# Seven block products for the down projections of two feed-forwards

## The chip, the cores and the metric

The kernel runs on one core of a Trainium2 chip. The metric is device time in microseconds (us), the median of several executions. TensorE (PE) does the matmuls, VectorE (DVE) and ScalarE (ACT) the elementwise work, GpSimd (POOL) little here, and SyncE's queue (SP) starts most of the transfers.

## The reference

One decoder layer on 512 tokens of width 1024, all in float32. The parts that matter here are the two feed-forwards, each with inner width 2816:

```
def swiglu(x, w_gate, w_up, w_down):
    return (jax.nn.silu(x @ w_gate) * (x @ w_up)) @ w_down

h = h + 0.5 * swiglu(rmsnorm(h, ffn1_norm), ffn1_w_gate, ffn1_w_up, ffn1_w_down)
... # mixer: sliding-window attention and gated linear attention, then h = h + concat(...) @ w_out
h = h + 0.5 * swiglu(rmsnorm(h, ffn2_norm), ffn2_w_gate, ffn2_w_up, ffn2_w_down)
h = h + sigmoid(rmsnorm(h, ple_gate_norm) @ ple_w_gate) * rmsnorm(p @ ple_w_proj, ple_norm)
```

## The kernel before

Every float32 factor of a large matmul is held as two float32r parts, high and low, whose sum is the value. A product is three matmuls (`mm3`): high x high, high x low, low x high. One matmul is 128 rows of contraction by 128 stationary columns by 512 moving columns, and accumulates in a PSUM bank of 512 float32 columns. There are eight banks, in three sets: `psA` (2), `psT` (4), `psG` (2).

Weights come through the class `Weights`. A list of units, in the order of use, is loaded by SP into raw tiles (two buffers of 128 x 2048), and each raw tile is split into ring tiles of 128 x 1024: ACT casts the high part (L87, `whi`), DVE subtracts it to get the low part (L88, `wlo`). The ring holds five high and five low tiles. A cast into a ring tile waits until PE has finished with the tile that had the slot. `get` asks for splits up to four units ahead of the one it returns.

`ffn` goes through the 22 blocks of 128 inner columns in three groups of 8, 8 and 6 (`GROUPS`). For each pair of blocks it computes gate and up for all 512 tokens, 24 matmuls for each of the four (8 contraction blocks x 3), into the four `psT` banks. The output has the inner columns on the partitions. Then `silu` on ACT (L267), the product with up on DVE (L269, `af`), the cast of the high part on ACT (L272, `ahi`), and the low part on DVE (L273, `alo`). At the end of a group comes the down projection: for each half of 512 output columns and each of the four token tiles, all blocks of the group accumulate in one `psA` bank, and one DVE instruction (L286) adds half of it to `h`. In the last group, `done(t)` follows a token tile's second half: it normalises the tile for the next stage, and the norm's transposes on PE come one tile later.

The program is written in order of use; a builder then fixes each engine's order of instructions by that order and by the times at which it reckons their inputs to be there. On the chip every engine takes its queue in that order.

Of the kernel before, what the change touches and what calls it, by code (L numbers as in the profile page):

```python
# [8 lines left out]
F32 = mybir.dt.float32  # L9
# [6 lines left out]
P = 128  # L16
# [9 lines left out]
GROUPS = ((0, 8), (8, 16), (16, 22))  # L26


class Weights:
    """Streams weight units from DRAM and splits each into two float32r parts whose sum is the float32 weight."""  # L30

    def __init__(self, nc, rawp, ringp, ahead):
        self.nc, self.rawp, self.ringp, self.ahead = nc, rawp, ringp, ahead
        self.units, self.where, self.tiles = [], {}, {}
        self.done = self.loaded = 0
        self.raws = []

# [5 lines left out]
    def add_cols(self, name, w, c0, nf):  # L43
        """[1024, nf*128] columns: one ring tile [P, 8, 128] per 128 columns."""
        keys = [(name, c0 // P + i) for i in range(nf)]
        src = w[:, c0:c0 + nf * P].rearrange("(k p) c -> p k c", p=P)
        self.add(keys, [P, KC, nf * P], [(slice(0, P), src)], [
            (lambda r, i=i: r[:, :, i * P:(i + 1) * P]) for i in range(nf)])

    def add_rows(self, name, w, k0, nk, c0, n, tag=None):  # L50
        """nk row blocks of 128 by n columns: one ring tile [P, 2, n] per two row blocks."""
        src = w[k0 * P:(k0 + nk) * P, c0:c0 + n].rearrange("(k p) c -> p k c", p=P)
        keys = [(name, c0 if tag is None else tag, k0 + i) for i in range(0, nk, 2)]
        self.add(keys, [P, nk, n], [(slice(0, P), src)], [
            (lambda r, i=i: r[:, i:i + 2, :]) for i in range(0, nk, 2)])

    def load(self):
        nc = self.nc
        keys, shape, loads, views = self.units[self.loaded]
        n = shape[1] * shape[2]  # L60
        u = self.loaded
        self.loaded += 1
        raw_t = self.rawp.tile([P, 2048], F32, name=f"wraw{u}", tag="wraw")
        raw = raw_t[:, :n].rearrange("p (k c) -> p k c", k=shape[1])
        for sl, src in loads:
            d = raw
            if isinstance(sl, tuple):
                d, sl = raw[:, :, sl[1]], sl[0]
            self.last_dma = nc.sync.dma_start(out=d[sl], in_=src).ins
        self.raws.append(raw)  # L70

    def split(self):
        nc = self.nc
        u = self.done
        while self.loaded <= u:
            self.load()
        keys, shape, loads, views = self.units[u]
        raw = self.raws[u]
        self.done += 1
        for i, (k, view) in enumerate(zip(keys, views)):  # L80
            v = view(raw)
            a, b = v.shape[1], v.shape[2]
            hi_t = self.ringp.tile([P, 1024], F32R, name=f"whi{u}_{i}", tag="whi")
            lo_t = self.ringp.tile([P, 1024], F32R, name=f"wlo{u}_{i}", tag="wlo")
            hi = hi_t[:, :a * b].rearrange("p (a b) -> p a b", a=a)
            lo = lo_t[:, :a * b].rearrange("p (a b) -> p a b", a=a)
            nc.scalar.copy(hi, v)  # L87
            (nc.gpsimd if u in (2, 3) else nc.vector).tensor_tensor(lo, v, hi.bitcast(F32), op=ALU.subtract)  # L88
            self.tiles[k] = (hi, lo)
# [8 lines left out]
def hymba_kernel(tc, A, out):  # L98
# [30 lines left out]
    def mm3(o, l, r, start, stop_):  # L129
        """o += l.T @ r where l and r are (hi, lo) pairs."""  # L130
        mm(o, l[0], r[0], start, False)
        mm(o, l[0], r[1], False, False)
        mm(o, l[1], r[0], False, stop_)

# [1 line left out]
    idn = cst.tile([P, P], F32, name="idn")  # L136
    make_identity(nc, idn)
    nhalf = cst.tile([P, 16], F32, name="nhalf")
# [13 lines left out]
    def add_ffn(i):  # L152
        g, u, d = A[f"ffn{i}_w_gate"], A[f"ffn{i}_w_up"], A[f"ffn{i}_w_down"]
        for f0, f1 in GROUPS:
            for f in range(f0, f1, 2):
                W.add_cols(f"g{i}", g, f * P, 2)
                W.add_cols(f"u{i}", u, f * P, 2)
            for c0 in (0, 512):
                for f in range(f0, f1, 4):
                    W.add_rows(f"d{i}", d, f, min(4, f1 - f), c0, 512)  # L160
# [84 lines left out]
    def ffn(i, nT, p, done, rest=None):  # L245
        first = True
        for f0, f1 in GROUPS:
            acts = {}
            for fa in range(f0, f1, 2):
# [4 lines left out]
                for a, b in halves:  # L254
                    if first and a and rest:
                        rest()
                    for j in range(2):
                        for m in range(2):
                            wh, wl = wts[j][m]
                            for k in range(KC):  # L260
                                mm3(pss[j][m][:, a:b], (wh[:, k, :], wl[:, k, :]),
                                    (nT[0][:, k, a:b], nT[1][:, k, a:b]), k == 0, k == KC - 1)
                first = False
                for j, f in enumerate(fs):
                    pg, pu = pss[j]
                    sg = p.tile([P, S], F32, name=f"sg{i}_{f}", tag="sg", bufs=2)
                    nc.scalar.activation(sg, pg, AF.Silu)  # L267
                    af = p.tile([P, S], F32, name=f"af{i}_{f}", tag="af", bufs=2)
                    nc.vector.tensor_mul(af, pu, sg)  # L269
                    ahi = p.tile([P, S], F32R, name=f"ahi{i}_{f}", tag="ahi", bufs=8)  # L270
                    alo = p.tile([P, S], F32R, name=f"alo{i}_{f}", tag="alo", bufs=8)
                    nc.scalar.copy(ahi, af)  # L272
                    nc.vector.tensor_sub(alo, af, ahi.bitcast(F32))  # L273
                    acts[f] = (ahi, alo)
            for c0 in (0, 512):
                tiles = [W.get((f"d{i}", c0, f)) for f in range(f0, f1, 2)]
                for t in range(NT):
                    ps = psA(f"pd{i}_{f0}_{c0}_{t}")
                    for j, (wh, wl) in enumerate(tiles):
                        for q in range(2):  # L280
                            f = f0 + 2 * j + q
                            ah, al = acts[f]
                            mm3(ps, (ah[:, tokens(t)], al[:, tokens(t)]), (wh[:, q, :], wl[:, q, :]),
                                f == f0, f == f1 - 1)
                    hs = h[t][:, c0:c0 + 512]
                    nc.vector.scalar_tensor_tensor(hs, ps, 0.5, hs, ALU.mult, ALU.add)  # L286
                    if c0 and f1 == NF:
                        done(t)

# [86 lines left out]
    with tc.tile_pool(name="ffn1p", bufs=1, reuse_waits="tile") as fp:  # L376
# [12 lines left out]
        ffn(1, nT1, fp, after1)  # L389

# [14 lines left out]
    def head_scale(src, name):  # L405
        """Per row and head of 64: (sum of squares + 64 eps) ** -0.5"""
# [7 lines left out]
    def rotate(x, tab, wide, name):  # L414
        """Rotary embedding of x (views by wide) with the gains folded into the tables."""
# [9 lines left out]
    # keys, values and gate ranks of all tokens  # L425
# [21 lines left out]
    # log decays of the recurrence and their running sums within chunks of 128 tokens  # L447
# [27 lines left out]
    # sliding-window attention; query heads are kept as pairs (h, h + 4), one per key head  # L475
# [73 lines left out]
    # gated linear attention  # L549
# [32 lines left out]
    # decayed scores of each chunk, transposed, by halving: pairs split at the middle of blocks of 2s tokens  # L582
# [51 lines left out]
    # decayed queries, keys and the state after each chunk  # L634
# [135 lines left out]
    hp = hpool.enter_context(tc.tile_pool(name="hp2", bufs=1, reuse_waits="tile"))  # L770
    h = [hp.tile([P, D], F32, name=f"h2_{t}") for t in range(NT)]
    for t in range(NT):
        nc.gpsimd.dma_start(out=h[t], in_=h_d[t])
    with tc.tile_pool(name="ffn2p", bufs=1, reuse_waits="tile") as fp:
        g2 = gain_tile("ffn2_norm")
        nT2 = norm_pair(fp, "f2")
# [13 lines left out]
        nT3 = norm_pair(xp, "pg")  # L790
# [7 lines left out]
        ffn(2, nT2, fp, after2, lambda: norm_transpose(*pend2[NT - 1]))  # L798

# [32 lines left out]
def _constants():  # L832
    """Tables that depend on the shapes alone: rotary angles and masks."""
# [46 lines left out]
```

## Time and profile before

| | before |
|---|---|
| median of 3 runs | 1035.73 us (1035.29 to 1036.16) |
| profiled execution, first to last instruction (its span) | 1034.1 us |
| PE busy | 1020.0 us |
| DVE busy | 457.8 us |
| ACT busy | 352.9 us |

The profile records one execution, and gives its time as the span alone; the difference of 1.6 us to the median is what lies around the span. Matmuls are pipelined: the profile's duration of one (some 390 ns) is longer than the step from one to the next, so that the step is read from a run of many.

### The profile page before, as it was taken

The numbers are of one execution on the slowest core, as the hardware profiler recorded it, in microseconds if no ns is written. First come the engines' busy times: TensorE is split into PE (matmuls) and PEld (weight loads), VectorE is DVE, ScalarE is ACT, GpSimd is POOL, SyncE is SP. The second block draws the span as 40 slices with busy tenths as digits, with TensorE's granted clock in tenths as the row PEclk, the third lists the DMA queues.
The fourth block names the chain that finished last, engine by engine and source line by source line (L and its number), as shares of the span: only waits on it lengthen the run. The fifth ranks groups of instructions, "written<-read, shape, count | busy, mean of one in ns | idle before, by whom it ended". The sixth has DMA issues, their size and how long they took to land.

```text
span 1034.1 us, 12380 instructions
## 1 busy us (share of the span) xinstructions
PE 1020.0 (99%) x5210; PEld 840.9 (81%) x5210; DVE 457.8 (44%) x610; ACT 352.9 (34%) x559; POOL 45.9 (4%) x58
## 2 busy tenths in 40 slices
PE   7999999999999999999999999999999999999998
PEld 5988888888888889887667779888888888888887
DVE  5533224333343346577876464332343323432553
ACT  6533113321132225554465243221132311332441
POOL 3300000000000001100000110000000000000100
PEclk9999999999999999999999999999999999999999
DMA  6842223322233234130203323332242222423231
GB/s 243 273 137 82 82 82 126 118 82 82 82 123 102 82 114 153 42 123 4 79 22 82 123 89 110 107 96 68 82 158 86 84 79 82 138 86 102 90 145 52
DMA packets 78203, 105.78 MB, mean 102 GB/s; under 512 B 5682, under 2 KB 55107, under 8 KB 78147
## 3 DMA queue, kind: packets, MB, share of 16 engines
q1 hardware_dynamic: 75842, 96.60, 28.6%
q0 software_dynamic: 2304, 8.39, 2.2%
q8 instruction: 41, 0.67, 0.3%
q14 instruction: 16, 0.12, 0.0%
HBM read 98.69 MB, written 6.29 MB: 102 GB/s over the span
## 4 chain that ended last, share of the span: by engine, by line
PE 97%; DVE 1%; ACT 1%; DMA 0%; issue 0%; SPq 0%
PE pg L127 23%; PE pu L127 23%; PE pd L127 23%; PE pgt L127 4%; PE wo L127 4%; PE gog L127 2%; PE gv L127 2%; PE gqk L127 2%; PE aq L127 2%; PE gr L127 1%; PE sc L127 1%; PE pv L127 1%; PE kvr L127 1%; PE o L127 1%; PE pe L127 1%; PE pt L540 1%
## 5 line engine op out<-in xcount | busy, mean ns | idle before, releaser
L87 ACT CAST whi<-wraw 128x1024 fp32r<-128x1024 f32 (+1 forms) x170 | 176.5, 1043 | 505.8 <-PE pg L127 144.7
L88 DVE TENSOR_TENSOR wlo<-wraw,whi 128x1024 fp32r<-128x1024 f32 (+1 forms) x166 | 200.5, 1212 | 215.1 <-ACT whi L87 205.4
L127 PE MATMUL pg<-nhi_f,whi 128*128 128x512 f32 (+1 forms) x384 | 143.3, 373 | 2.3 <-ACT nhi_f L196 2.3
L127 PE MATMUL pg<-nlo_f,whi 128*128 128x512 f32 (+1 forms) x384 | 143.6, 374 | 0.0
L127 PE MATMUL pu<-nhi_f,whi 128*128 128x512 f32 (+1 forms) x384 | 142.8, 372 | 0.5 <-DVE h L784 0.5
L127 PE MATMUL pg<-nhi_f,wlo 128*128 128x512 f32 (+1 forms) x384 | 143.1, 373 | 0.0
L127 PE MATMUL pu<-nlo_f,whi 128*128 128x512 f32 (+1 forms) x384 | 142.8, 372 | 0.0
L127 PE MATMUL pu<-nhi_f,wlo 128*128 128x512 f32 (+1 forms) x384 | 142.6, 371 | 0.0
L127 PE MATMUL pd<-whi,ahi 128*128 128x512 f32 x352 | 137.3, 390 | 0.2
L127 PE MATMUL pd<-wlo,ahi 128*128 128x512 f32 x352 | 137.0, 389 | 0.0
L127 PE MATMUL pd<-whi,alo 128*128 128x512 f32 x352 | 136.0, 389 | 0.0
L269 DVE TENSOR_TENSOR af<-pu,sg 128x512 f32<-128x512 f32 x44 | 30.4, 691 | 137.1 <-PE pu L127 136.7
L127 PEld LDWEIGHTS pg<-nhi_f,whi 128*128 128x128 f32 x384 | 72.7, 189 | 15.3 <-ACT nhi_f L196 3.0
L127 PEld LDWEIGHTS pu<-nhi_f,whi 128*128 128x128 f32 x384 | 72.5, 189 | 13.1 <-DVE h L784 0.7
L127 PEld LDWEIGHTS pg<-nhi_f,wlo 128*128 128x128 f32 x384 | 72.9, 190 | 12.6
L127 PEld LDWEIGHTS pg<-nlo_f,whi 128*128 128x128 f32 x384 | 72.8, 190 | 12.6 <-DVE nlo_f L197 0.2
L127 PEld LDWEIGHTS pu<-nlo_f,whi 128*128 128x128 f32 x384 | 72.5, 189 | 12.5
L127 PEld LDWEIGHTS pu<-nhi_f,wlo 128*128 128x128 f32 x384 | 72.3, 188 | 12.5
L286 DVE SCALAR_TENSOR_TENSOR h<-pd,h 128x512 f32<-128x512 f32 x48 | 33.1, 689 | 108.8 <-PE pd L127 108.8
L127 PEld LDWEIGHTS pd<-whi,ahi 128*128 128x128 f32 x352 | 66.1, 188 | 14.6 <-DVE h L286 1.1
L127 PEld LDWEIGHTS pd<-whi,alo 128*128 128x128 f32 x352 | 66.1, 188 | 13.8
L127 PEld LDWEIGHTS pd<-wlo,ahi 128*128 128x128 f32 x352 | 66.1, 188 | 13.6
(228 smaller groups left out, 1167.6 us busy)
## 6 DMA issues: line engine op xcount, KB each, us to landing
wraw<-in_ffn_w_gate_dram SPq DMA_DIRECT2D x22, 1024.0 KB, 5.1
wraw<-in_ffn_w_up_dram SPq DMA_DIRECT2D x22, 1024.0 KB, 5.2
wraw<-in_ffn_w_down_dram SPq DMA_DIRECT2D x20, 1024.0 KB, 5.0
wraw<-in_w_in_dram SPq DMA_DIRECT2D x8, 1024.0 KB, 5.2
wraw<-in_ple_w_gate_dram SPq DMA_DIRECT2D x4, 1024.0 KB, 5.3
h<-in_x_dram SPq DMA_DIRECT2D x4, 512.0 KB, 8.5
emb_d<-eo POOLq DMA_DIRECT2D x4, 512.0 KB, 4.6
wraw<-in_ffn_w_down_dram SPq DMA_DIRECT2D x4, 512.0 KB, 3.5
```

What stands on the lines that cost most here:

```text
L87: nc.scalar.copy(hi, v)
L88: (nc.gpsimd if u in (2, 3) else nc.vector).tensor_tensor(lo, v, hi.bitcast(F32), op=ALU.subtract)
L127: nc.tensor.matmul(o, lhsT=l, rhs=r, start=start, stop=stop_, **kw)
L269: nc.vector.tensor_mul(af, pu, sg)
L286: nc.vector.scalar_tensor_tensor(hs, ps, 0.5, hs, ALU.mult, ALU.add)
L540: nc.tensor.transpose(pt[:, tokens(a)], e[:, a, kb * P:(kb + 1) * P], idn)
```

## The change

The down projection of a group becomes a two-by-two block product done with seven products in place of eight. The activations are cut into token halves (tiles 0 and 1; tiles 2 and 3) and, in a group, into even and odd blocks; the weights into even and odd row blocks and left and right output halves. Sums of blocks are the factors: four additions or subtractions of 256 columns for each pair of activation blocks (`cb`, slots 0 to 6), and four subtractions of weight blocks for each group, done in place in the raw pair. All seven activation factors of a pair are cast together (`acts_hi[:, j]`) and get their low parts together (`acts_lo[:, j]`). Each product is 256 tokens by 512 columns, in one bank for each of two token tiles; products 2, 3 and 4 go on accumulating in the banks of 1, 5 and 7, after these have been read. Sums that all groups share are kept in `U` and added to `h` in the last group.

The groups become six: five with two pairs of blocks and one, (4, 6), with one. In a feed-forward the ring gets two more slots (`xwhi`, `xwlo`: seven in all). A group's down weights are loaded as one pair of tiles, even and odd blocks, with a single buffer. In the second feed-forward this buffer and the high parts lie where the mixer's transposed inputs lay; the norms' transposes move to a pool of their own.

```diff
-GROUPS = ((0, 8), (8, 16), (16, 22))
+GROUPS = ((0, 4), (4, 6), (6, 10), (10, 14), (14, 18), (18, 22))
+ORDER = ((1, 0), (5, 1), (2, 2), (3, 6), (7, 5), (6, 4), (4, 3))
+ORDER_LAST = ((1, 0), (5, 1), (2, 2), (3, 6), (6, 4), (7, 5), (4, 3))
...
+    def add_products(self, name, w, f0, f1, order):
+        nk = (f1 - f0) // 2
+        for n, (q, _) in enumerate(order):
+            self.add([(name, q, f0)], [P, nk, 512], (w[f0 * P:f1 * P, :], n == 0), q)
+    def ring(self, name, tag, key):
+        pool, t = self.ringp, tag
+        if self.extra is not None and key[0] in ("g1", "u1", "d1", "g2", "u2", "d2") and self.turn % (5 + self.extra[1]) >= 5:
+            pool, t = self.extra[0], "x" + tag
+        return pool.tile([P, 1024], F32R, name=name, tag=t, **({} if pool is self.ringp else {"bufs": self.extra[1]}))
+    def load_pair(self, u, w, nk):
+        src = w.rearrange("(k two p) c -> two p k c", p=P, two=2)
+        self.pair = []
+        for j in range(2):
+            t = self.raw2(f"wpr{u}_{j}", j)[:, :nk * 1024].rearrange("p (k c) -> p k c", k=nk)
+            self.last_dma = self.nc.sync.dma_start(out=t, in_=src[j]).ins
+            self.pair.append(t)
+        return self.pair
...
+        if isinstance(views, int):
+            ev, od = raw
+            b11, b12, b21, b22 = ev[:, :, 0:512], ev[:, :, 512:1024], od[:, :, 0:512], od[:, :, 512:1024]
+            v, sub = {1: (b11, None), 2: (b21, None), 3: (b22, None), 4: (b21, (b21, b11)), 5: (b11, (b12, b11)),
+                      6: (b11, (b22, b11)), 7: (b12, (b12, b22))}[views]
+            if sub:
+                nc.vector.tensor_sub(v, *sub)
+            views, raw = [lambda r: r], v
...
+            hi_t = self.ring(f"whi{u}_{i}", "whi", k)
+            lo_t = self.ring(f"wlo{u}_{i}", "wlo", k)
...
-            for c0 in (0, 512):
-                for f in range(f0, f1, 4):
-                    W.add_rows(f"d{i}", d, f, min(4, f1 - f), c0, 512)
+            W.add_products(f"d{i}", d, f0, f1, ORDER_LAST if f1 == NF else ORDER)
...
+        U = [p.tile([P, 512], F32, name=f"U{i}_{b}") for b in range(2)]
+        acts_hi = hi_p.tile([P, 2, 7, 256], F32R, name=f"ahi{i}", tag="nlo")
+        acts_lo = p.tile([P, 2, 7, 256], F32R, name=f"alo{i}")
+        raws = [raw_p.tile([P, 4096], F32, name=f"draw{i}", tag="nhi")]
+        W.raw2 = lambda name, j: raws[0][:, j * 2048:(j + 1) * 2048]
+        W.extra = (p, n_extra)
...
-                    nc.vector.tensor_mul(af, pu, sg)
-                    nc.scalar.copy(ahi, af)
-                    nc.vector.tensor_sub(alo, af, ahi.bitcast(F32))
+                cb = p.tile([P, 7, 256], F32, name=f"cb{i}_{fa}", tag="cb", bufs=1)
+                    nc.vector.tensor_mul(cb[:, 2 * q:2 * q + 2, :].rearrange("p a c -> p (a c)"), pu, sg)
+                nc.vector.tensor_sub(cb[:, 5, :], cb[:, 1, :], cb[:, 0, :])
+                nc.vector.tensor_add(cb[:, 1, :], cb[:, 1, :], cb[:, 3, :])
+                nc.vector.tensor_sub(cb[:, 4, :], cb[:, 1, :], cb[:, 0, :])
+                nc.vector.tensor_sub(cb[:, 6, :], cb[:, 2, :], cb[:, 4, :])
+                nc.scalar.copy(acts_hi[:, j], cb)
+                nc.vector.tensor_sub(acts_lo[:, j], cb, acts_hi[:, j].bitcast(F32))
+            banks = {}
+            for q, slot in (ORDER_LAST if last else ORDER):
+                wh, wl = W.get((f"d{i}", q, f0))
+                for b in range(2):
+                    onto = {2: 1, 3: 5, 4: 7}.get(q)
+                    ps = banks[onto, b] if onto else (psA if q in (1, 7) else psG)(f"pd{i}_{f0}_{q}_{b}")
+                    banks[q, b] = ps
+                    for k in range(nk):
+                        mm3(ps, (acts_hi[:, k, slot, tokens(b)], acts_lo[:, k, slot, tokens(b)]),
+                            (wh[:, k, :], wl[:, k, :]), k == 0 and not onto, k == nk - 1, skip_group_check=onto is not None)
...
+                    if q in (1, 6):
+                        if f0 == 0 and q == 1:
+                            nc.scalar.copy(U[b], ps)
+                        else:
+                            nc.vector.tensor_add(U[b], U[b], ps)
+                    if q == 2:
+                        half_add(h1[:, l], ps)
+                    elif q in (5, 7):
+                        half_add(h2[:, r], ps)
+                    elif q == 3:
+                        half_add(h1[:, r], ps)
+                    elif q == 4:
+                        half_add(h2[:, l], ps)
+                    if last and q == 6:
+                        half_add(h1[:, r], U[b])
+                        done(b)
+                        half_add(h2[:, l], U[b])
+                        half_add(h2[:, r], U[b])
+                    if last and q == 4:
+                        done(2 + b)
```

## Rows read from the trace of the kernel before

**Rows 1.** The page: one engine line, and the granted clock in 40 slices.

```profile
PE 1020.0 (99%) x5210; PEld 840.9 (81%) x5210; DVE 457.8 (44%) x610; ACT 352.9 (34%) x559; POOL 45.9 (4%) x58
...
PEclk9999999999999999999999999999999999999999
```

**Rows 2.** The chain that ended last, in order of time: start, us, what.

```profile
111.80 5.44 PE pu L127 x24
117.24 43.52 PE pd L127 x192
...
386.48 4.09 PE pd L127 x18
390.58 0.25 PE kvr L127 x2
...
404.09 1.39 PE aq L127 x6
405.48 1.50 PE kvr L127 x12
```

**Rows 3.** Waits: engine, line, waited for: us in total, times, longest.

```profile
ACT whi L87 <- PE pg L127: 144.7, 42, 4.5
...
DVE h L286 <- PE pd L127: 108.8, 30, 4.8
...
PE pg L127 <- ACT nhi_f L196: 2.3, 3, 1.8
```

**Rows 4.** DMA issues of the page: queue, count, size, median us to landing.

```profile
wraw<-in_ffn_w_down_dram SPq DMA_DIRECT2D x20, 1024.0 KB, 5.0
```

**Rows 5.** Groups by line and form: busy us, mean ns of one, idle before.

```profile
L88 DVE TENSOR_TENSOR wlo<-wraw,whi 128x1024 fp32r<-128x1024 f32 x162 | 197.8, 1225 | 215.1 <-ACT whi L87 205.4 <-PE qtr L495 2.2
L87 ACT CAST whi<-wraw 128x1024 fp32r<-128x1024 f32 x166 | 173.9, 1052 | 504.5 <-PE pg L127 144.7 <-PE pd L127 124.4 <-issue 84.2
...
L286 DVE SCALAR_TENSOR_TENSOR h<-pd,h 128x512 f32<-128x512 f32 x48 | 33.1, 689 | 108.8 <-PE pd L127 108.8
...
L197 DVE TENSOR_TENSOR nlo_mix<-ntr_mx,nhi_mix 128x512 fp32r<-128x512 f32 x8 | 5.5, 690 | 3.6 <-ACT nhi_mix L196 3.6
...
L216 DVE SCALAR_TENSOR_TENSOR nrm_mx<-h,rs_mx,gain_mix_norm 128x1024 f32<-128x1024 f32 x4 | 5.1, 1282 | 1.6 <-POOL rs_mx L203 1.5
...
L88 DVE TENSOR_TENSOR wlo<-wraw,whi 128x544 fp32r<-128x544 f32 x4 | 2.8, 719 | 0.0
...
L87 ACT CAST whi<-wraw 128x544 fp32r<-128x544 f32 x4 | 2.6, 647 | 1.4 <-PE pd L127 1.4
```

**Rows 6.** Timeline of DVE in the mixer, two dependent operations: start, us.

```profile
414.36 0.42 DVE L421 TENSOR_TENSOR r_k<-kn,rsn 128x256 f32<-128x256 f32 x1
414.81 0.69 DVE L422 TENSOR_TENSOR r_k<-r_k 128x512 f32<-128x512 f32 x1
```

**Rows 7.** Timeline, the first group's step from up to down.

```profile
117.06 1.06 ACT L87 CAST whi<-wraw 128x1024 fp32r<-128x1024 f32 x1 [3.89 <-PE pu L127]
117.08 0.39 PE L127 MATMUL pd<-whi,ahi 128*128 128x512 f32 x1
...
117.35 0.69 DVE L269 TENSOR_TENSOR af<-pu,sg 128x512 f32<-128x512 f32 x1 [3.42 <-PE pu L127]
...
118.08 0.62 ACT L272 CAST ahi<-af 128x512 fp32r<-128x512 f32 x1
118.14 1.23 DVE L88 TENSOR_TENSOR wlo<-wraw,whi 128x1024 fp32r<-128x1024 f32 x1
...
119.28 0.69 DVE L273 TENSOR_TENSOR alo<-af,ahi 128x512 fp32r<-128x512 f32 x1
```

**Rows 8.** Timeline of PE near the start; in brackets the idle time before.

```profile
24.82 0.39 PE L127 MATMUL pg<-nhi_f,whi 128*128 128x256 f32 x1 [1.83 <-ACT nhi_f L196]
```

**Rows 9.** Windows of 1 us; after the engines: PEclk, DMA share, GB/s.

```profile
27.00:28.00 1.00, 1.00 (x6) 1.00 (x6) 0.00 (x0) 1.00 (x4) 0.98 (x3) 0.50 0.15 29
...
30.00:31.00 1.00, 1.00 (x10) 1.00 (x9) 0.07 (x1) 0.90 (x3) 1.00 (x2) 0.93 1.06 415
```

More of the change, by code (lines that the diff above doesn't have):

```diff
@@ L36, in __init__ @@
         self.raws = []
+        self.pair = None
+        self.extra, self.turn = None, 0
     def add(self, keys, shape, loads, views, after=None):
@@ L59, in load @@
         keys, shape, loads, views = self.units[self.loaded]
+        if isinstance(views, int):
+            w, first = loads
+            self.raws.append(self.load_pair(self.loaded, w, shape[1]) if first else self.raws[-1])
+            self.loaded += 1
+            return
         n = shape[1] * shape[2]
@@ L79, in split @@
         self.done += 1
+        if isinstance(views, int):
+            ev, od = raw
[5 more added lines that the diff above has]
+            views, raw = [lambda r: r], v
         for i, (k, view) in enumerate(zip(keys, views)):
@@ L82, in split @@
             a, b = v.shape[1], v.shape[2]
-            hi_t = self.ringp.tile([P, 1024], F32R, name=f"whi{u}_{i}", tag="whi")
-            lo_t = self.ringp.tile([P, 1024], F32R, name=f"wlo{u}_{i}", tag="wlo")
+            hi_t = self.ring(f"whi{u}_{i}", "whi", k)
+            lo_t = self.ring(f"wlo{u}_{i}", "wlo", k)
+            self.turn += 1
             hi = hi_t[:, :a * b].rearrange("p (a b) -> p a b", a=a)
@@ L127, in mm, with mm3 @@
         nc.tensor.matmul(o, lhsT=l, rhs=r, start=start, stop=stop_, **kw)
[L129 to L133, printed above, removed]
+    def mm3(o, l, r, start, stop_, **kw):
+        mm(o, l[0], r[0], start, False, **kw)
+        mm(o, l[0], r[1], False, False, **kw)
+        mm(o, l[1], r[0], False, stop_, **kw)
     idn = cst.tile([P, P], F32, name="idn")
     make_identity(nc, idn)
-    nhalf = cst.tile([P, 16], F32, name="nhalf")
+    nhalf = cst.tile([P, 8], F32, name="nhalf")
     nc.gpsimd.memset(nhalf, -0.5)
@@ L243, in gemm_ts, with ffn, half_add @@
                     k == 0, k == 2 * n - 1)
-    def ffn(i, nT, p, done, rest=None):
+    def ffn(i, nT, p, done, hi_p, raw_p, n_extra, rest=None):
         first = True
+        U = [p.tile([P, 512], F32, name=f"U{i}_{b}") for b in range(2)]
[4 more added lines that the diff above has]
+        W.extra = (p, n_extra)
+        def half_add(hs, x):
+            nc.vector.scalar_tensor_tensor(hs, x, 0.5, hs, ALU.mult, ALU.add)
         for f0, f1 in GROUPS:
-            acts = {}
-            for fa in range(f0, f1, 2):
+            last = f1 == NF
+            nk = (f1 - f0) // 2
+            for j, fa in enumerate(range(f0, f1, 2)):
                 fs = (fa, fa + 1)
@@ L256, in ffn @@
                         rest()
-                    for j in range(2):
+                    for q in range(2):
                         for m in range(2):
-                            wh, wl = wts[j][m]
+                            wh, wl = wts[q][m]
                             for k in range(KC):
-                                mm3(pss[j][m][:, a:b], (wh[:, k, :], wl[:, k, :]),
+                                mm3(pss[q][m][:, a:b], (wh[:, k, :], wl[:, k, :]),
                                     (nT[0][:, k, a:b], nT[1][:, k, a:b]), k == 0, k == KC - 1)
@@ L263, in ffn @@
                 first = False
-                for j, f in enumerate(fs):
-                    pg, pu = pss[j]
+                cb = p.tile([P, 7, 256], F32, name=f"cb{i}_{fa}", tag="cb", bufs=1)
+                for q, f in enumerate(fs):
+                    pg, pu = pss[q]
                     sg = p.tile([P, S], F32, name=f"sg{i}_{f}", tag="sg", bufs=2)
                     nc.scalar.activation(sg, pg, AF.Silu)
-                    af = p.tile([P, S], F32, name=f"af{i}_{f}", tag="af", bufs=2)
-                    nc.vector.tensor_mul(af, pu, sg)
-                    ahi = p.tile([P, S], F32R, name=f"ahi{i}_{f}", tag="ahi", bufs=8)
-                    alo = p.tile([P, S], F32R, name=f"alo{i}_{f}", tag="alo", bufs=8)
-                    nc.scalar.copy(ahi, af)
-                    nc.vector.tensor_sub(alo, af, ahi.bitcast(F32))
-                    acts[f] = (ahi, alo)
@@ L275, in ffn @@
[L275 to L288, printed above, removed]
+                    nc.vector.tensor_mul(cb[:, 2 * q:2 * q + 2, :].rearrange("p a c -> p (a c)"), pu, sg)
@@ new lines, in ffn @@
+                nc.vector.tensor_sub(cb[:, 5, :], cb[:, 1, :], cb[:, 0, :])
[14 more added lines that the diff above has]
+                            (wh[:, k, :], wl[:, k, :]), k == 0 and not onto, k == nk - 1, skip_group_check=onto is not None)
+                    h1, h2 = h[b], h[2 + b]
+                    l, r = slice(0, 512), slice(512, 1024)
+                    if q in (1, 6):
[18 more added lines that the diff above has]
+                        done(2 + b)
@@ L291, in hymba_kernel @@
+        W.extra = None
     emb_d = [drp.tile([P, D], F32, name=f"emb_d{t}") for t in range(NT)]
@@ L387, in after1 @@
                 norm_transpose(*pend[t - 1])
-        ffn(1, nT1, fp, after1)
+        ffn(1, nT1, fp, after1, fp, fp, 2)
     hpool.close()
@@ L773, in hymba_kernel @@
         nc.gpsimd.dma_start(out=h[t], in_=h_d[t])
+    np_ = hpool.enter_context(tc.tile_pool(name="nt2p", bufs=1, reuse_waits="tile"))
     with tc.tile_pool(name="ffn2p", bufs=1, reuse_waits="tile") as fp:
         g2 = gain_tile("ffn2_norm")
-        nT2 = norm_pair(fp, "f2")
+        nT2 = norm_pair(np_, "f2")
         pend2 = []
@@ L789, in hymba_kernel @@
         g3 = gain_tile("ple_gate_norm")
-        nT3 = norm_pair(xp, "pg")
+        nT3 = norm_pair(np_, "pg")
         pend3 = []
@@ L796, in after2 @@
                 norm_transpose(*pend3[t - 1])
-        ffn(2, nT2, fp, after2, lambda: norm_transpose(*pend2[NT - 1]))
+        ffn(2, nT2, fp, after2, xp, xp, 2, lambda: norm_transpose(*pend2[NT - 1]))
     with tc.tile_pool(name="outp", bufs=1, reuse_waits="tile") as op:
```

## Prediction

> **What bounds the kernel now.** I read the page first. TensorE (PE) is busy for 1020.0 of 1034.1 us, VectorE (DVE) for 44%, ScalarE (ACT) for 34%, and the granted clock is full in all 40 slices [rows 1]. The chain that ended last, in order of time, is PE almost throughout: 192 down-projection matmuls take 43.52 us, so 226.7 ns each, and the 24 matmuls of one gate or up block take 5.44 us, the same 226.7 ns [rows 2]. The view of waits shows why nothing else matters yet: ACT and DVE wait for PE, by hundreds of us, and PE's longest wait after its first load is 1.8 us [rows 3]. ACT's cast into the weight ring waits for PE to release a slot; the ring is always full and the next tile is cast when a slot comes free. So the time is the number of matmuls, plus any hole that the change puts into PE's queue.
>
> **What is removed.** Per feed-forward the old down projection issues 2 column halves x 4 token tiles x 22 row blocks x 3 = 528 matmuls of 512 columns. The new one issues 7 products x 2 token tiles x 11 block pairs x 3 = 462. Two feed-forwards: 132 fewer, x 226.7 ns = **29.9 us off PE**. All are 128x128 against 512 columns as before, so I take the old spacing.
>
> The rows give that spacing from 192 matmuls in one unbroken run [rows 2]. The Trainium skill ("TensorE: Matmul & The Clock Gate", Back-to-back issue gap) gives about 131 ns for a sustained stream at 512 columns; by it 132 matmuls are worth 17.3 us, an estimate from that page, and the sum below would end 12.6 us higher, at 1053. The trace disagrees with it, and the measurement decides; it gets no chance of its own.
>
> **What is added, and its cover.** The span is 1034.1 us; the runs' median is 1035.73, so 1.6 us lies around the span and I keep it.
>
> Weights: as many bytes as before, in two loads per group, each landing in about the 5.0 us of the old loads [rows 4]. The pair buffer is single: in SP's queue the next pair's two loads wait until the last product of the group before is split, near that group's first product, and the gate and up loads of the group after stand behind them. The next pair's first split comes with a slot that is released four products later (10.9 us), and those gate loads are needed later still. No cost; uncovered it would be two landings, 10 us per group. In the second feed-forward this buffer and the activations' high parts take the place of the mixer's transposes, free when the output projection ends; the first pair is needed eight gate and up blocks (43.5 us) later. No cost either.
>
> DVE, per feed-forward: the old down tiles' 22 splits become 42 product splits, 7 of them half-wide (35 x 1.225 + 7 x 0.72 - 22 x 1.225 = +21.0 us [rows 5]); 24 block sums of weights come on top, 4 half-wide (20 x 1.225 + 4 x 0.72 = +27.4, taken like a split of that size); activations need four 256-column sums per pair of blocks (44 x 0.42 [rows 6] = +18.5) and one 1792-column low part (2.03, below) in place of two of 0.69 (+7.2); drains rise from 24 to 88 reads at 0.69 us [rows 5] (+44.2). Together some 118 us; twice that on 457.8 [rows 1] is 694, 67% of the span. ACT gains about 24 each, by the same rows. Neither becomes the bound on average: PE's 43.5 us of gate and up per two-pair group hide this work, except where a chain stands in front of PE; uncovered, it would be the 118.
>
> **The chain in front of each group's products.** Let T be the start of the first matmul after the last up matmul (117.08 in rows 7). Before, the multiply starts 0.27 us after T, the cast follows at 1.00, and the low part's subtract ends at 2.9, behind one weight split [rows 7]; 15 matmuls (3.4 us) of older blocks covered that. After the change the same path is: multiply, 0.27 to 0.96; then three dependent 256-column operations (S1, S2, A12-S2), whose step in a dependent sequence is 0.45 us [rows 6], to 2.3; one cast of all seven factors, 1792 columns. The cast has no row; by the slope between 544 and 1024 elements (0.647 and 1.052 us, so 0.844 ns each [rows 5]) it is 1.70 us: high parts at **T+4.05**. The low subtract by its slope (0.719 and 1.225, 1.054 ns each [rows 5]) is 2.03 us: low parts at **T+6.1**.
>
> What can PE do meanwhile? Products 1 and 5 have fresh banks for two token tiles each: four banks, and of each the three matmuls of the older pair: 12 matmuls, 2.72 us. Product 2 accumulates onto product 1's bank, after that is drained; 3 and 4 likewise. The next group's gate needs a ring slot, and the seven slots hold six product tiles, with the seventh entering at T. So PE waits, and with it the rest of its queue: the products, and the next gate behind them, whose banks ACT and DVE wait for.
> - two-pair groups: 4.05 - 2.72 = 1.3 us; then eight matmuls on high parts (1.8 us, to 5.9), 0.2 until the low parts; product 1's first bank ends at 6.3, its drain needs 0.27 + 0.69 and ends at 7.3, while PE has work until 7.0: 0.3. **1.8 us each, ten groups: 18 us.** Floor 1.3 (13 us). Ceiling, if the issue order, which is fixed when the kernel is built, has all three matmuls of a bank in a row: high parts at 4.05, two matmuls, then idle from 4.5 to 6.1: 3.2 each, 32 us. I take 1.8, since the builder places instructions by when their inputs are due and the trace of before has almost no PE waits [rows 3].
> - the one-pair group (4, 6): no older pair, nothing to cover: 4.05 + 0.2 + 0.3, and 0.3 where drains lag (14 drains of 0.69 are 9.7 us beside 9.5 us of matmuls, with weight splits between, until the next gate's first tile is in the ring and fills PE). **4.8 each, two groups: 9.7 us.** Floor 4.05 (8.1); ceiling, if four splits of 1.22 queue ahead of drains, 8.8 (17.6).
>
> Clock: after a PE gap of 1.8 us near the start [rows 8] the trace shows the granted clock fall from full (2.4 GHz) to 0.50 (1.2 GHz) and come back within the 31st us [rows 9]; about 3.4 us at half speed, 1.7 lost. Waits of 4 us are longer than that gap, so I charge both one-pair groups: **3.4 us**. Two-pair gaps of 1.3 us are shorter: nothing, ceiling 10 x 1.7 = 17.
>
> Ends of the feed-forwards: before, four norms follow row tiles 4.1 us apart (18 matmuls) and PE goes straight into the next stage, with the last key/value matmuls at 405.5 [rows 2]. After, two of four token tiles finish only with product 4, 1.4 us apart, and six extra additions of 0.69 us stand in DVE's queue with the drains, between the norms. DVE's list from product 6 to the last norm (12 drains or additions 8.3, norm scalings 5.1, low parts 5.5, first weight splits 2.9) is 21.8 us [rows 5], of which 6.8 pass under the last five bank groups of 1.36: it ends some 15 us after the last product; before, the last norm's columns were used 14.9 us after it (405.5 - 390.6 [rows 2]). So little is lost: **3.5 us for both ends**, floor 0, ceiling 7.
>
> **Sum.** -29.9 + 18 + 9.7 + 3.4 + 3.5 = +4.7 us: span 1038.8, time **1040.4**. The saving is eaten by holes.
>
> **Rivals.**
> - *PE fills the holes* (faster). One mechanism: a slot of the ring is free early enough that the next group's gate matmuls run in the wait before the high parts. If all of 1.3 x 10 + 4.05 x 2 = 21 us is filled, the clock doesn't fall either and the time is 1016; it decides from about 7 us of filling. For it: PE before does run other work when one input is late (six query matmuls ahead of the last key/value ones [rows 2]). Against: every tile is cast when a slot is released [rows 3], in the order of use, and seven products use up seven slots. To this side belong also floors of all terms together: 1027.
> - *The low parts come late in a fixed order* (slower). PE's queue is served in order; if a wlo split or the block sums delay the 2 us subtract, or three matmuls of a bank stand in a row, each two-pair group pays 3.2 instead of 1.8: +14 us, 1054; with the clock falling in each group, 1071. For it: in the trace a 1.23 us split already runs ahead of the low subtract [rows 7]. Against: DVE idles while ACT casts, so a split fits there.
> - *DVE becomes the bound.* It would need over 95%; the sum gives 67%. Only the one-pair group comes near, and that is in its term.
>
> **Numbers.** Forecast and its neighbourhood (1033.7 to 1048): 0.50. Holes filled, in part or all, or all floors (1006 to 1033.7): 0.34. Late order or clock falls in most groups (1048 to 1072): 0.16. Within 0.2% (1033.7 to 1037.8), about what a measurement of this kernel can tell from no change: 0.16 out of the first, which leaves 0.34 of it slower. Range 1024 to 1055: it leaves out the deep part of the filled case and the clock falling everywhere, about 0.1 each, by halves of their cases. As cases of both signs hold much of the chance, the forecast's own range is 1034 to 1048.
>
> **What would show it.** PE busy falls by about 30 us while the span doesn't; the matmul count drops by 132; PE's waits name ACT's cast of the seven factors and DVE's low subtract at twelve places, 1.3 to 2 us in ten, over 4 us in two; the granted clock dips after the two. The prediction is wrong if these waits are under 1 us or absent, if PE runs gate matmuls between first products, or if DVE's weight splits rather than the activation chain are what PE waits for.

## The result and the profile after

The changed kernel takes **1071.96 us** (median of 4 runs, 1071.24 to 1072.59) beside 1035.95 us for the kernel before in the same session: a ratio of 1.0335, 95% interval 1.0312 to 1.0359. It is 36 us slower. The forecast was 1040.4 with a range up to 1055: the sign was right, the size far too small. The profiled execution has a span of 1070.6 us, 36.5 more than before, and this is the span that the lines below divide up.

The page's engine line and granted clock, to be read against [rows 1]:

```profile
PE 1013.6 (95%) x5078; PEld 824.7 (77%) x5078; DVE 675.3 (63%) x892; ACT 400.7 (37%) x581; POOL 48.6 (5%) x58
...
PEclk9999999999999989999999999998999999999899
```

132 matmuls fewer, as counted, but PE is busy only 6.4 us less, and the clock is no longer full in every slice. DVE has 217 us more work and is still idle for a third of the span. PE's waits, of which [rows 3] show the longest before (2.3 us in total, after the first load), are now led by these:

```profile
PE pd L170 <- ACT ahi L327: 31.2, 12, 4.4
PE pd L170 <- DVE h L296: 9.6, 2, 6.3
```

Twelve waits for the cast of the activation factors, one per row group, and two for a drain, one at the end of each feed-forward. The chain of work shows that the matmuls themselves have kept their step: 24 of up still take 5.45 us, as in [rows 2], while the first 24 products behind the third group's wait take 7.38 in place of 5.44. The last row is a later piece of the same group at full clock:

```profile
171.70 5.45 PE pu L170 x24
182.10 7.38 PE pd L170 x24
195.37 5.44 PE pd L170 x24
```

The terms that [rows 4, 5] gave by slopes and by counts:

```profile
draw<-in_ffn_w_down_dram SPq DMA_DIRECT2D x20, 1024.0 KB, 5.6
```

```profile
L120 DVE TENSOR_TENSOR draw<-draw 128x1024 f32<-128x1024 f32 x40 | 48.9, 1222 | 0.8
L328 DVE TENSOR_TENSOR alo<-cb,ahi 128x1792 fp32r<-128x1792 f32 x22 | 44.5, 2025 | 34.1 <-ACT ahi L327 34.1
...
L324 DVE TENSOR_TENSOR cb<-cb 128x256 f32<-128x256 f32 x22 | 9.3, 424 | 0.6
...
L327 ACT CAST ahi<-cb 128x1792 fp32r<-128x1792 f32 x22 | 37.1, 1688 | 47.8 <-DVE cb L326 47.8
```

The cast was forecast at 1.70 us and takes 1.69; the low part 2.03 and takes 2.03; a weight sum 1.225 and takes 1.22. The durations are right. What was wrong is their place, as the timeline of the first group shows (start, duration, engine; to be laid beside [rows 7]):

```profile
73.42 0.39 PE L170 MATMUL pd<-whi,ahi 128*128 128x512 f32 x1
...
73.69 0.69 DVE L322 TENSOR_TENSOR cb<-pu,sg 128x512 f32<-128x512 f32 x1 [0.34 <-PE pu L170]
...
74.42 0.43 DVE L324 TENSOR_TENSOR cb<-cb 128x256 f32<-128x256 f32 x1
...
74.76 1.22 DVE L131 TENSOR_TENSOR wlo<-draw,whi 128x1024 fp32r<-128x1024 f32 x1
...
75.89 0.42 DVE L325 TENSOR_TENSOR cb<-cb 128x256 f32<-128x256 f32 x1
...
76.35 0.42 DVE L326 TENSOR_TENSOR cb<-cb 128x256 f32<-128x256 f32 x1
76.81 1.68 ACT L327 CAST ahi<-cb 128x1792 fp32r<-128x1792 f32 x1 [2.36 <-DVE cb L326]
78.52 2.02 DVE L328 TENSOR_TENSOR alo<-cb,ahi 128x1792 fp32r<-128x1792 f32 x1 [1.75 <-ACT ahi L327]
...
78.54 0.50 PE L170 MATMUL pd<-whi,ahi 128*128 128x512 f32 x1 [2.24 <-ACT ahi L327]
```

T is 73.42. A weight split of 1.22 us stands in DVE's queue between two sums of the chain, so the high parts come at T+5.1 and not at T+4.05, and PE's hole is 2.24 us instead of 1.3. The split stands at this place in all ten two-pair groups, and one place earlier, ahead of the first sum, in both one-pair groups; the hole is 2.24 in the ten, and 4.42 in the two.

Windows around the third group's wait (PE busy and count, PEld, DVE, ACT, POOL, then the granted clock, DMA share, GB/s):

```profile
180.00:182.10 2.10, 0.00 (x0) 0.00 (x0) 0.35 (x2) 1.68 (x1) 0.00 (x0) 1.00 0.70 183
182.20:183.30 1.10, 1.10 (x5) 0.92 (x6) 1.10 (x1) 0.00 (x0) 0.00 (x0) 1.00 1.01 417
183.50:186.70 3.20, 3.20 (x9) 2.43 (x8) 2.03 (x4) 1.00 (x2) 0.00 (x0) 0.50 0.07 28
187.00:190.00 3.00, 3.00 (x15) 2.44 (x14) 3.00 (x5) 1.14 (x2) 0.00 (x0) 1.00 0.00 0
```

The same columns in the second one-pair group, whose products start at 731.73:

```profile
729.60:731.70 2.10, 0.00 (x0) 0.00 (x0) 0.36 (x1) 1.68 (x1) 0.00 (x0) 0.50 0.84 261
731.80:736.30 4.50, 4.50 (x11) 3.53 (x12) 2.26 (x2) 0.00 (x0) 0.00 (x0) 0.50 0.26 105
```

In the third group PE stands, starts again, and only then, some 1.3 us later, the clock goes to its lower level (1.2 GHz). In that stretch matmuls start 427 ns apart instead of 227: eight of them lose 1.6 us. In the second one-pair group, and at both ends, the clock has fallen before PE starts again. It falls in four of the ten two-pair groups (1.1 to 1.3 us behind the restart), in both one-pair groups and at both ends; in all, 80 product matmuls took 33.8 us by their starts, 15.6 more than at full clock: about 10.8 at group starts and 4.8 at the ends.

Where the clock stays up, PE makes two short stops behind the hole, for the low parts and for the first drain. Two weight loads of PE in the fourth group, whose hole ends at 248.84, show them; the matmuls started 0.11 and 0.25 us late:

```profile
250.89 0.76 PEld L170 LDWEIGHTS pd<-whi,alo 128*128 128x128 f32 x4 [0.37 <-DVE alo L328]
252.17 0.19 PEld L170 LDWEIGHTS pd<-whi,ahi 128*128 128x128 f32 x1 [0.52 <-DVE U L345]
```

With a slower first step after the hole and after each stop (337 ns in place of 227), the first 24 products lose 0.75 us on average in the six such groups. In the four groups where the clock fell, they lose 1.76: at the slower step PE does not run into the two stops. Beside the same hole a fall thus costs 1.0 us net.

The end of the second feed-forward, where PE waits 6.35 us:

```profile
1005.83 3.69 DVE L296 SCALAR_TENSOR_TENSOR h<-U,h 128x512 f32<-128x512 f32 x6
...
1009.43 1.22 DVE L131 TENSOR_TENSOR wlo<-wraw,whi 128x1024 fp32r<-128x1024 f32 x1
1010.57 0.16 DVE L255 SCALAR_TENSOR_TENSOR ms_pg<-ss_pg 128x1 f32<-128x1 f32 x1
1010.64 1.29 DVE L296 SCALAR_TENSOR_TENSOR h<-pd,h 128x512 f32<-128x512 f32 x2
...
1011.38 0.79 PE L170 MATMUL pd<-whi,ahi 128*128 128x512 f32 x1 [6.35 <-DVE h L296]
```

Product 4 accumulates in product 7's bank; that bank's drain (`h<-pd`, 1010.64) stands in DVE's queue behind six additions of `U` and a weight split for the next stage.

Put together, against the span before: -29.9 for the matmuls; +31.2 of holes before the products, and about 6 for the short stops and slower first steps behind them (844 product matmuls at full clock start 235.3 ns apart on average, 227.7 before); +10.5 of holes at the ends (3.26, 6.35 and 0.93); +15.6 of clock. That is +33.4 of the 36.5; of the last 3 us, about half lies in the transposes and gate matmuls at the ends, and the rest is spread thinly.

### The profile page after: what moved, and what is told of

Read it like the earlier page. It is cut to its first block, busy times and chain, and to the rows that moved or that the text cites. A ratio compares the mean times of both kernels' runs of the same rounds, so it can differ in the third digit from the quotient of the medians.

```text
span 1070.6 us, 12431 instructions
## 1 busy us (share of the span) xinstructions
PE 1013.6 (95%) x5078; PEld 824.7 (77%) x5078; DVE 675.3 (63%) x892; ACT 400.7 (37%) x581; POOL 48.6 (5%) x58
## 4 chain that ended last, share of the span: by engine, by line
PE 87%; DVE 7%; ACT 4%; DMA 1%; issue 1%; POOL 0%; SPq 0%; DVEq 0%; POOLq 0%; ACTq 0%
PE pg L170 23%; PE pu L170 22%; PE pd L170 17%; PE pgt L170 4%; PE wo L170 3%; PE gv L170 2%; PE aq L170 2%; PE gqk L170 2%; ACT ahi L327 2%; DVE wlo L131 2%; PE gog L170 2%; PE gr L170 1%; PE sc L170 1%; PE pv L170 1%; PE pe L170 1%
## 5 line engine op out<-in xcount | busy, mean ns | idle before, releaser
L130 ACT CAST whi<-wraw 128x1024 fp32r<-128x1024 f32 (+1 forms) x126 | 128.6, 1038 | 191.2 <-PE pd L170 125.6
L130 ACT CAST whi<-draw 128x1024 fp32r<-128x1024 f32 (+1 forms) x84 | 82.3, 981 | 272.2 <-PE pg L170 112.5
L131 DVE TENSOR_TENSOR wlo<-wraw,whi 128x1024 fp32r<-128x1024 f32 (+1 forms) x122 | 145.8, 1205 | 47.5 <-ACT whi L130 44.5
L170 PE MATMUL pd<-whi,ahi 128*128 128x512 f32 x308 | 128.3, 416 | 41.4 <-ACT ahi L327 31.2
L131 DVE TENSOR_TENSOR wlo<-draw,whi 128x1024 fp32r<-128x1024 f32 (+1 forms) x84 | 95.0, 1133 | 74.8 <-ACT whi L130 74.6
L170 PE MATMUL pd<-wlo,ahi 128*128 128x512 f32 x308 | 125.5, 408 | 0.0
L170 PE MATMUL pd<-whi,alo 128*128 128x512 f32 x308 | 120.2, 411 | 0.0
L170 PEld LDWEIGHTS pd<-whi,ahi 128*128 128x128 f32 x308 | 60.8, 197 | 63.3 <-ACT ahi L327 36.3
L296 DVE SCALAR_TENSOR_TENSOR h<-pd,h 128x512 f32<-128x512 f32 x120 | 79.8, 687 | 29.6 <-PE pd L170 29.1
L322 DVE TENSOR_TENSOR cb<-pu,sg 128x512 f32<-128x512 f32 x44 | 30.4, 691 | 92.2 <-PE pu L170 91.6
```

Source lines behind the costliest of these rows:

```text
L170: nc.tensor.matmul(o, lhsT=l, rhs=r, start=start, stop=stop_, **kw)
L296: nc.vector.scalar_tensor_tensor(hs, x, 0.5, hs, ALU.mult, ALU.add)
L322: nc.vector.tensor_mul(cb[:, 2 * q:2 * q + 2, :].rearrange("p a c -> p (a c)"), pu, sg)
```

## The experiments

Theory: PE waits for one long chain per group (product, sums, one cast of everything), and the clock loss hangs on these holes. Rivals were that the regrouping or the drains cost the time, that DVE's queue at the ends is the loss, and that clock and holes are independent. Times are medians, and ratios are to the kernel before in the same session.

**1. Fill the holes with matmuls nobody reads.** Nothing is left out; a bank is written and never used.

```diff
+            fill = psT(f"fill{i}_{f0}")
+            for z in range(10 if nk == 2 else 20):
+                jj = 2 - nk
+                mm(fill, acts_hi[:, jj, 0, 0:P], acts_hi[:, jj, 0:2, :], True, True)
```

> The changed kernel with ten matmuls (twenty in the one-pair group) that no output uses, given to PE's queue after each group's products, where they fall into the wait for the factors' cast. Their result is thrown away; nothing of the computation is left out. Theory clock: about half of the added loss is not the waits but the half-speed stretches behind them, 41 us at 1.2 GHz in all. The waits at the twelve group starts stay as long (hidden under the extra matmuls), the seven slow stretches of 3.4 us there go, and about 12 us come back: 1060. Rival: the clock falls for another reason, and the slow stretches stay: 1072. Rival: the extra matmuls run longer than the holes and push the products back: 1074 or more.

Measured: 1066.45 us, ratio 1.0299 (1.0284 to 1.0314). Waits of PE:

```profile
PE pd L170 <- DVE h L296: 9.6, 2, 6.3
...
PE pd L170 <- ACT ahi L327: 0.8, 1, 0.8
```

The holes at group starts are gone, and with them every fall of the clock at these places; those at the start of the kernel and at the two ends stay. So the falls come from the holes. The size was missed: 5.5 us instead of 12. By the starts of the matmuls, the clock's loss in products goes from 15.6 to 4.9 (-10.7), but the fillers take 33.4 us where gaps of 29.6 vanish (+3.8), and the products' other starts cost 1.6 more. That is 5.3 of the 5.5.

**2. Move the additions of U to the second half of `h` behind product 7's drain**, in the last group.

```diff
                     if last and q == 6:
                         half_add(h1[:, r], U[b])
                         done(b)
+                    if last and q == 7:
                         half_add(h2[:, l], U[b])
                         half_add(h2[:, r], U[b])
```

> The changed kernel with four of the six additions of U in the last group moved from behind product 6 to behind product 7's drains. Theory ends: PE's waits of 3.3 and 6.4 us before product 4 come from product 7's drains standing behind these additions in DVE's queue; both waits go, with the two slow stretches of 6.8 us that follow them: 9.6 plus some 6, so about 1056. Rival: DVE has the same work to do before the norms, and the lost time only moves to the norms and the next stage: 1066 to 1070. By the working of the prediction, which saw the norms as what is late there: 1068.

Measured: 1073.84 us, ratio 1.0364 (1.0348 to 1.038): no gain. The expected 1056 was missed, and all three figures lie below the result. Waits of PE:

```profile
PE ntr_pg L264 <- DVE nrm_pg L257: 7.4, 1, 7.4
...
PE ntr_mx L264 <- DVE nrm_mx L257: 3.6, 1, 3.6
...
PE ntr_mx L264 <- DVE nlo_mix L238: 1.8, 1, 1.8
```

Both waits for the drain are gone and stand again, as large, before the norms' transposes: the rival's mechanism. This new order of DVE's work at the ends only moves the loss. That less work there would remove it, this run does not show; see run 6.

**3. Cast the first two factors alone**, as soon as the first sum is there; the other five after the rest of the sums.

```diff
                 nc.vector.tensor_add(cb[:, 1, :], cb[:, 1, :], cb[:, 3, :])
+                nc.scalar.copy(acts_hi[:, j, 0:2], cb[:, 0:2])
+                nc.vector.tensor_sub(acts_lo[:, j, 0:2], cb[:, 0:2], acts_hi[:, j, 0:2].bitcast(F32))
                 nc.vector.tensor_sub(cb[:, 4, :], cb[:, 1, :], cb[:, 0, :])
                 nc.vector.tensor_sub(cb[:, 6, :], cb[:, 2, :], cb[:, 4, :])
-                nc.scalar.copy(acts_hi[:, j], cb)
-                nc.vector.tensor_sub(acts_lo[:, j], cb, acts_hi[:, j].bitcast(F32))
+                nc.scalar.copy(acts_hi[:, j, 2:7], cb[:, 2:7])
+                nc.vector.tensor_sub(acts_lo[:, j, 2:7], cb[:, 2:7], acts_hi[:, j, 2:7].bitcast(F32))
```

> The changed kernel with the factors of products 1 and 5 (slots 0 and 1) cast and split by themselves as soon as their sum is there, and the other five after. Theory chain: the hole at each group start is the path to one cast of all seven factors. The first two high parts should be there 2.1 us after the last up matmul instead of 5.1, inside the 2.7 us of older matmuls: no wait in the ten two-pair groups, some 2 us in the one-pair groups, and few falls of the clock there. 1035 to 1040. Rival DVE: it is DVE that is behind (63% busy, splits between the sums), and two more DVE instructions for each pair of blocks gain nothing: 1065 or more.

Measured: 1036.28 us, ratio 1.0003 (0.9994 to 1.0012): 35.7 us back, with two instructions more per pair. Its timeline of ACT in the first group, and PE's waits:

```profile
74.50 0.62 ACT L325 CAST ahi<-cb 128x512 fp32r<-128x512 f32 x1 [0.43 <-DVE cb L324]
76.91 1.26 ACT L329 CAST ahi<-cb 128x1280 fp32r<-128x1280 f32 x1 [1.79 <-DVE cb L328]
```

```profile
PE pd L170 <- DVE h L296: 9.6, 2, 6.3
PE pd L170 <- ACT ahi L325: 4.9, 2, 2.4
```

The weight split still stands between the sums, but the first products no longer wait for what comes after it: the two-pair holes are gone, the one-pair holes are 2.44. All gaps on PE after the first load together fall from 48.1 to 23.5 us, and the clock's loss in products from 15.6 to 6.8; the products' other starts give the rest. The Trainium skill (Perfetto Trace Analysis, Optimizing Scalar/DVE Operations) says that where ScalarE or VectorE is not saturated but makes another engine wait, breaking up its instructions may let the work finish sooner. The runs agree: ACT was at 37%.

**4. Begin with products that need no late sum.** The order becomes 1, 7, 2, 5, 6, 3, 4. Product 7 uses a difference within the first block of a pair, so the first two factors are cast while the second block's up matmuls still run; the others follow in three casts. Product 5 gets `psT` banks, and its weight sum is taken right after product 1's split, because product 7 overwrites the block it needs. In the last group the additions of `U` to `h2` come after product 3. These changes were made together and not run apart.

```diff
-ORDER = ((1, 0), (5, 1), (2, 2), (3, 6), (7, 5), (6, 4), (4, 3))
+ORDER = ((1, 0), (7, 4), (2, 2), (5, 1), (6, 5), (3, 6), (4, 3))
...
+                    if q == 0:
+                        nc.vector.tensor_sub(cb[:, 4, :], cb[:, 1, :], cb[:, 0, :])
+                        parts(slice(0, 5, 4))
+                parts(slice(2, 4))
+                nc.vector.tensor_add(cb[:, 1, :], cb[:, 1, :], cb[:, 3, :])
+                parts(slice(1, 2))
+                nc.vector.tensor_sub(cb[:, 5, :], cb[:, 1, :], cb[:, 0, :])
+                nc.vector.tensor_sub(cb[:, 6, :], cb[:, 2, :], cb[:, 5, :])
+                parts(slice(5, 7))
```

`parts` casts a slice of slots and subtracts its low part.

> Seven products in the order 1, 7, 2, 5, 6, 3, 4: the factors of the first two come from the older blocks of each pair and are cast before the last up matmul ends; three casts in place of one; product 5 uses the gate banks; the additions of U in the last group stand behind product 3's drains. Theory (chain, ends and clock together are the whole loss): no PE waits at group starts, none before product 4, no fall of the clock after the start: the 29.9 us of matmuls appear, less a few: 1006 to 1013. Rival: the seven-product form is held by DVE (some 690 us of work and more drains): 1035 or more. Rival: only the chain, not the ends: about 1022.

Measured: 1024.81 us, ratio 0.9885 (0.9856 to 0.9913): 11 us faster than the kernel before. The expected 1006 to 1013 was missed; the rival that named about 1022, with the ends left as they were, came nearest. No hole is left at any group start; the ends have kept theirs:

```profile
PE ntr_mx L267 <- DVE nrm_mx L260: 5.4, 1, 5.4
PE ntr_pg L267 <- DVE nrm_pg L260: 4.8, 1, 4.8
```

The clock falls at both. In this profile it also fell for 10.2 us in the output projection, at 566 us:

```profile
566.30:576.30 10.00, 10.00 (x26) 7.33 (x27) 4.12 (x9) 1.24 (x4) 2.37 (x3) 0.50 0.01 2
```

From the first matmul of `wo` on, 32 matmuls took 11.0 us there and 6.6 in the kernel before: 4.4 us. PE's hole there is 0.7 us, and 0.7 before as well, so why it fell is open. The four runs lie at 1021.7, 1022.1, 1027.5 and 1027.5, and the profiled one is of the upper pair; the lower pair's mean granted clock is higher (0.993 and 0.991 beside 0.986), which fits executions without this fall, but no profile shows them.

**5. The six row groups alone**: the kernel before, with its eight products.

```diff
-GROUPS = ((0, 8), (8, 16), (16, 22))
+GROUPS = ((0, 4), (4, 6), (6, 10), (10, 14), (14, 18), (18, 22))
```

> The kernel before with its eight products, in the six row groups alone (no sums of blocks, the same 5210 matmuls). Theory (the long chain of sums and the one cast of all seven factors makes the waits): each group waits only for the old short chain, 0 to 0.5 us in a two-pair group and about 1.5 in a one-pair group: 1037 to 1046, and few slow stretches. Rival (six drains of h and six starts in place of three are the loss, not the sums): holes of 2 us or more in all twelve groups, 1060 to 1070.

Measured: 1037.24 us, ratio 1.0013 (0.9993 to 1.0033): no difference. PE waits for a drain twice, 0.6 us at most, and never for a cast of activations:

```profile
PE pd L127 <- DVE h L286: 1.1, 2, 0.6
```

More starts and 48 more drains cost nothing; what the groups paid in the changed kernel came with the sums.

**6. No U in the last group.** As 4, but the last group of each feed-forward by the eight old products, and `U` added to `h` at the end of the group before. These are two edits at once; they were not run apart.

```diff
+            if last:
+                for c0 in (0, 512):
+                    tiles = [W.get((f"d{i}", c0, f)) for f in range(f0, f1, 2)]
...
+                                    mm3(pd[t], (acts_hi[:, j, sl, tokens(t % 2)], acts_lo[:, j, sl, tokens(t % 2)]),
+                                        (wh[:, q, :], wl[:, q, :]), j == 0 and q == 0, j == nk - 1 and q == 1)
...
+            if f1 + 4 == NF:
+                for b in range(2):
+                    half_add(h[b][:, 512:], U[b])
+                    half_add(h[2 + b][:, :512], U[b])
+                    half_add(h[2 + b][:, 512:], U[b])
```

> As the run with the early casts (1024.8 us), but the last row group of each stage by the eight old products, with the sums U added into h at the end of the group before. Theory (what is left at the two ends, holes of 5.4 and 4.8 us and the slow stretches behind them, comes from the additions of U and the drains that stand before the norms on VectorE): both holes close to under 1 us, 24 more matmuls cost 5.4 us, the slow stretches at 378 and 969 us go (about 4 us by the excess of the matmuls in them): 1012 to 1018. Rival (the norms of the next stage wait there whatever the products are, as the additions moved behind product 7 showed): the holes stay and only the matmuls are added: 1028 to 1032.

Measured: **1011.41 us**, ratio 0.9769 (0.9735 to 0.9802). Its page, and the longest of PE's waits after the first load:

```profile
PE 995.5 (99%) x5102; PEld 820.7 (81%) x5102; DVE 641.6 (64%) x908; ACT 400.3 (40%) x633; POOL 45.7 (5%) x58
...
PEclk9999999999999999999999999999999999999999
```

```profile
PE pg L173 <- ACT nhi_f L244: 2.3, 3, 1.9
```

The holes at the ends are gone, and the waits are those of [rows 3] again. Which of the two edits closed them is not shown. It has 108 matmuls fewer than before: 108 x 226.7 ns is 24.5 us, and the runs are 24.6 us faster. With every new hole closed, the saving by count is the saving in time, although DVE has 184 us more work than before.

**7. The cast done twice in a row**, with nothing left out: 1.7 us more on the chain.

```diff
                 nc.scalar.copy(acts_hi[:, j], cb)
+                nc.scalar.copy(acts_hi[:, j], cb)
```

> The changed kernel with ScalarE's cast of all seven factors done twice in a row, 1.7 us more on the chain of each pair group. Theory (the chain of sums and cast is what TensorE waits for, and a longer wait drops its clock in more groups): every hole grows by 1.7 us (two-pair 2.24 to 3.9, one-pair 4.4 to 6.1), 20 us over twelve groups, and the six two-pair groups that kept the high clock lose it too, each 1 to 1.5 us: 1096 to 1104 against 1072. Rival 1 (holes alone, the clock does not follow them): 1090 to 1094. Rival 2 (the cast is not on the path): 1071 to 1076.

Measured: 1101.74 us, ratio 1.0632 (1.0604 to 1.0659), 29.8 us over the changed kernel.

```profile
PE pd L170 <- ACT ahi L328: 52.0, 12, 6.1
```

The twelve holes grow by 20.8 us together (nearly all two-pair ones from 2.24 to 3.96, one-pair ones from 4.42 to 6.14: 1.72 for 1.68 of cast). The clock now falls in all ten two-pair groups instead of four, and its loss in products goes from 15.6 to 24.7 us. Beside that, with the clock down in every group, the short stops behind the holes get fewer: all steps of the products together, holes aside, grow by 7.0. The 20.8 and 7.0, with about 1 us elsewhere, make up the 28.6 between the two profiled spans; the medians are 29.8 apart. Holes alone would have given some 1093.

## Why the prediction was wrong

- **Matmuls saved, 29.9 us: right.** 132 fewer at an unchanged step; the last version, with 108 fewer, shows such a count turn into time one for one. The Trainium skill (TensorE: Matmul & The Clock Gate, Back-to-back issue gap) has about 131 ns for that step; no run here shows it, and the last version gains by 226.7 per matmul.
- **The chain in front of the products: right in mechanism and in each duration, wrong in its order.** "DVE idles while ACT casts, so a split fits there" is the sentence that failed: the builder put the split between two sums, where it delays the cast. The 1.0 us of delay is read from the timeline; no run takes the split out of the chain. Each two-pair group pays a hole of 2.24 where 1.3 stood, and behind it about 0.5 by the average above, where 0.2 for the low parts and 0.3 for the drain stood (0.75 where the clock stayed up): some 27 us for the ten instead of 18. Run 7 shows that the chain passes into the hole one for one. The one-pair groups paid 4.42 and about 0.5 each, 9.8 in all where 9.7 stood. The first and the third group, whose timelines were read, did run the matmuls on high parts first, as assumed.
- **The clock, 3.4 us: the step that was mis-sized at the group starts.** It was charged to the one-pair groups alone, as two-pair holes were to stay under the 1.83 us of [rows 8]. At 2.24 they passed it, and four of ten fell: with the one-pair groups 10.8 us by the slow matmuls. Net of the short stops that these replaced it is less, 1.0 and not 1.6 for each of the four. Runs 1 and 7 show that the falls follow the holes.
- **The ends, 3.5 us: the largest miss.** 10.5 of holes and 4.8 of clock: 15.3. The prediction counted DVE's list to the last norm and compared its end with the time before, 15 us beside 14.9; no row gives the 3.5 that it then took. It left out that PE needs results from the middle of that list: product 4 waits for product 7's bank, whose drain is queued behind additions of `U` and a split of the next stage's weights; and with that drain put ahead (run 2), the norms' transposes wait as long. Run 6, with neither the seven products nor the additions of `U` at the end, has no hole.
- **DVE as the bound, regrouping, transfers: rightly left at nothing.** DVE reached 63% where 67% was reckoned; run 5 prices the groups at no difference, and no transfer is among PE's new waits.
- **Filled holes, the faster rival: did not happen.** No gate matmul ran in a hole. The slower rival, with the clock falling in each group, named 1071, but by another way: low parts late in a fixed order. What came late was the high parts, and the clock fell in six of twelve groups, so that its figure fits is chance.

In sum: 9 us from the split inside the chain, 7 from the clock behind it, 12 from the ends, and some 3 outside these terms: the 31.6 us between 1040.4 and 1072.0.

## What to carry over

When fewer matmuls are bought with sums, list what the first product of each group needs and cast only that first: one instruction that converts everything makes PE wait for the last sum. Price a chain with one foreign instruction of the same engine in its middle, since the queue's order is not yours, and price a hole also with the work behind it at half clock. At the end of a stage, look for the first result that PE needs from a loaded queue, not for when the queue runs empty.

## What the runs showed of the hardware

- The lower clock can come behind the hole or within it. In the third group PE stood until 182.10, ran five matmuls at the full step, and then eight at 427 ns; in the second one-pair group the clock fell 2.2 us before PE started again, and ten matmuls ran slow from the first. Beside the same hole of 2.24 us, a fall cost 1.0 us net over the next 24 products.
- The fall is not decided by the hole's length alone: the same 2.24 us hole was followed by one in four groups of ten; with the cast done twice, all ten of about 4 us were. A hole of 0.7 us saw one in run 4 and none in the kernel before.
- A matmul that starts PE again after a wait is dear by itself: behind each of the ten two-pair holes the next matmul started 336 to 338 ns later, and not 227. The products of the changed kernel outside the slow stretches start 235.3 ns apart on average, and those of the last version, without waits, 226.9.
